# Seven products for k-pairs 2 and 5, token sums made beside their operand, w_mix_out's second half in single blocks, weight splits of 2048 columns

## The chip, the cores and the metric

The kernel runs on one core of a Trainium2 chip. The metric is the device time of one execution in microseconds (us). The kernel before takes 2048.77 us, the median of three runs (2047.95 to 2048.99). The three lie within 1.04 us of one another.

Engines in the profile: PE is TensorE (matmuls), PEld its weight loads, DVE VectorE, ACT ScalarE, POOL GpSimd, SP SyncE, which here only issues transfers.

## The reference

One decoder layer on 256 tokens of 2048 features, with 256 memory tokens, all float32:

```python
hn = rmsnorm(h, norm_mix_w)
q, k, v, g_ret, xr, yr, g_a, g_b = split(hn @ w_in)          # 2048 x 14336
ret_out = silu(g_ret) * head_groupnorm(retention(rotary(q), rotary(k), v))
rnn_out = gelu(yr) * rg_lru(causal_dwconv(xr))
merged = sigmoid(g_a) * (ret_out @ w_proj_ret) + sigmoid(g_b) * (rnn_out @ w_proj_rnn)
h = h + merged @ w_mix_out
h = h + memory_cross_attention(rmsnorm(h), rmsnorm(mem), w_q, w_k, w_v, w_o)
gate, val = split(causal_dwconv(rmsnorm(h) @ w_up))           # 2048 x 11264
h = h + (silu(gate) * val) @ w_down                           # 5632 x 2048
return rmsnorm(h, final_norm_w)
```

All weight matrices are used once, for 256 tokens. They make up nearly all of the 388 MB that the profile shows read from HBM.

## The kernel before

**A product in three.** Each operand is split into hi (rounded to fp32r) and lo (the remainder), and a product is hi·hi + lo·hi + hi·lo, three matmuls of 128 x 128 x 512 (`mm`, L235; `products_n` and `rows_of`). The tokens are the stationary operand (128 features x 128 tokens), the weights the moving one (128 features x 512 columns).

**The weight stream.** `weight_plan` (L68) lists the products in order; `weight_stream` cuts each into chunks of 1 MB, four tiles of 128 x 512, which lie in that order in one DRAM array. `prefetch` (L257) issues the load of a chunk on SP into one of three buffers (`raw`) and then its split: ACT writes hi (a cast, L326 or L339), DVE subtracts for lo (L328 or L340). A split is made in halves of two tiles, 1024 columns, each in a buffer of its own (`hi` and `lo`, six of each, PART_BUFS). `chunks` (L360) keeps AHEAD = 2 chunks prefetched beyond the one being multiplied.

**Single blocks.** `steps_n`/`gemm_n` makes one block of 512 columns for both token halves (2 x 128): for 2048 features 16 feature tiles in four chunks, 24 matmuls each, 96 in all.

**Paired blocks.** `steps_pair`/`pair` (L442 to L501) makes two blocks at once, in eight steps, each a k-pair: two feature tiles x two column blocks, one chunk. A step takes the plain eight tile products (24 matmuls), or, where its number is in `seven`, seven products after Strassen's and Winograd's scheme (21 matmuls) on sums of blocks. For these the weights' sums are made by `seven_parts` (L343): split of p1, p3 (1024 columns) and p2 (512), four additions on DVE (L349), then the split of the sums, q, in two halves. The tokens' sums are made by `sums_of` (L421 to L440): g = hi + lo of the operand (DVE, L428), four differences tq of 128 columns (DVE, L436), their split ts (ACT L437, DVE L438). `steps_pair` asks for them up to two steps ahead. The paired stages are, in order: w_proj_rnn, w_in's gate A (GA), w_proj_ret and w_mix_out, two pairs each, with SEVEN = (1, 3, 5); xa_w_o's first pair with SEVEN_O = (3, 5), its other two blocks single; w_down's first two parts (FF_PARTS), two pairs each, with SEVEN.

**Where operands come from.** A result lies with tokens on partitions and is turned for the next product by `by_dma` (L512): ACT copies it into planes of 16-bit halves (pl, L520), SP issues two DMA transposes (pt), and a step or more later ACT joins the planes (f, L533); then `split_pair` (L549) or `split_cols` splits it into the operand of the next product. For w_proj_rnn the operand `rnn` is made in `gelu_y`, for w_proj_ret `ret` in `split_head` (L711), for w_mix_out `merged` in `turn_merged` (L938), for xa_w_o `osp` in `split_block` (L1044), for w_down `hid` in `gate_up` (L1104), after the convolutions (L1088, L1090). `residual` (L964) runs w_mix_out and xa_w_o and turns each block into the operand of the next stage; during w_mix_out it also squares and splits the memory tokens (`memory_steps`, L608). `pending`/`later` (L356) runs such work after a given number of steps.

**Order.** The program is written in a frame that assigns an order to each engine's instructions, by their dependencies and priorities; matmuls keep the order of the program. On each engine instructions are issued in that order, and one that waits holds those behind it.

Of the kernel before, what the change touches and what calls it, by code (L numbers as in the profile page):

```python
# [9 lines left out]
F32 = mybir.dt.float32  # L10
# [22 lines left out]
PART_BUFS = 6  # L33
# [8 lines left out]
SEVEN = (1, 3, 5)  # L42
# [25 lines left out]
def weight_plan():  # L68
# [81 lines left out]
def hybrid_layer(  # L150
# [106 lines left out]
    def prefetch(n):  # L257
        while len(ahead) < n and taken[0] < len(stream):
# [56 lines left out]
            parts = []  # L315
            for k in range(0, nk, KH):
                if own:
                    xs[k2 + k // KH]
                hi = wp.tile([P, KH, BW], F32R, tag="hi", bufs=PART_BUFS, name=nm("hi"))
                lo = wp.tile([P, KH, BW], F32R, tag="lo", bufs=PART_BUFS, name=nm("lo"))  # L320
                for cs in (slice(k, k + 1), slice(k + 1, k + 2)) if i < 4 else (slice(k, k + KH),):
                    ds = slice(cs.start - k, cs.stop - k)
                    if i == 0 and cs.start == 0:
                        dve.tensor_copy(hi[:, ds], raw[:, cs, :])
                    else:
                        act.copy(hi[:, ds], raw[:, cs, :])  # L326
                    with tc.issue_after(split[cs.start]) if i == 0 else nullcontext():
                        dve.tensor_tensor(  # L328
                            out=lo[:, ds], in0=raw[:, cs, :], in1=hi[:, ds].bitcast(F32), op=ALU.subtract
                        )  # L330
                parts.append((hi, lo))
            ahead.append(((row, c), parts))

    def weight_parts(src):

        n = src.shape[1]
        hi = wp.tile([P, KH, BW], F32R, tag="hi", bufs=PART_BUFS, name=nm("hi"))
        lo = wp.tile([P, KH, BW], F32R, tag="lo", bufs=PART_BUFS, name=nm("lo"))
        act.copy(hi[:, 0:n], src)  # L339
        dve.tensor_tensor(out=lo[:, 0:n], in0=src, in1=hi[:, 0:n].bitcast(F32), op=ALU.subtract)  # L340
        return [(hi[:, i, :], lo[:, i, :]) for i in range(n)]

    def seven_parts(raw):  # L343

        b12, b11, b22, b21 = (raw[:, i, :] for i in range(4))
        p1, p3 = weight_parts(raw[:, 1:3])
        (p2,) = weight_parts(raw[:, 3:4])
        for o, a, b in ((b11, b12, b11), (b12, b12, b22), (b22, b11, b22), (b21, b22, b21)):
            dve.tensor_tensor(out=o, in0=a, in1=b, op=ALU.add)  # L349
        q3, q1 = weight_parts(raw[:, 0:2])  # L350
        q2, q4 = weight_parts(raw[:, 2:4])
# [40 lines left out]
    def steps_n(w, row, st, nk, col):  # L392
# [3 lines left out]
        for k0, n, parts in chunks(nk, w, row, col):  # L396

            def tile_(tt, kk):
                k = k0 + kk
                hi, lo = (t[:, kk % KH, :] for t in parts[kk // KH])  # L400
# [20 lines left out]
    def sums_of(t):  # L421

        if id(t) not in token_sums:
            g = big([P, 2, 2, P], s="g")
            o = big([P, 2, 4, P], F32R, s="ts")
            s = tmp("tq").rearrange("p a (b n) -> p (a b) n", b=2)
            flat = g.rearrange("p j i n -> p j (i n)")
            dve.tensor_tensor(  # L428
                out=flat, in0=t[:, :, 0:S].bitcast(F32), in1=t[:, :, S:BW].bitcast(F32), op=ALU.add
            )  # L430
            (a11, a21), (a12, a22) = ([g[:, j, i, :] for i in range(2)] for j in range(2))
            for d, a, b, op in (
                (0, a21, a22, ALU.subtract), (2, a11, a21, ALU.subtract),
                (1, s[:, 0, :], a11, ALU.subtract), (3, a12, s[:, 1, :], ALU.add),
            ):
                dve.tensor_tensor(out=s[:, d, :], in0=a, in1=b, op=op)  # L436
            act.copy(o[:, 0], s)  # L437
            dve.tensor_tensor(out=o[:, 1], in0=s, in1=o[:, 0].bitcast(F32), op=ALU.subtract)  # L438
            token_sums[id(t)] = (t, o)
        return token_sums[id(t)][1]  # L440

    def steps_pair(w, row, st, nk, c1, c2, seven=SEVEN):  # L442
# [14 lines left out]
        for k0, n, parts in chunks(nk, w, row, (c1, c2, seven)):  # L457
            k2 = k0 // KH
            for i in seven:
                if k2 < i <= k2 + 2:  # L460
                    sums_of(st[i])
# [5 lines left out]
            if k2 in seven:  # L467
# [5 lines left out]
                s1, s2, s3, s4 = ((ts[:, 0, i, :], ts[:, 1, i, :]) for i in range(4))  # L473
# [14 lines left out]
            else:  # L488
                end = k0 + n == nk
                for b, names in enumerate((("p2", "p4"), ("x3", "n"))):  # L490
                    hi, lo = parts[b]
# [767 lines left out]
```

## Time and profile before

| | us |
|---|---|
| median of three runs | 2048.77 |
| the profiled execution | 2047.84 |
| its span, first to last instruction | 2046.1 |
| PE busy in the span | 1991.3 |
| DVE busy | 1542.0 |
| ACT busy | 1343.0 |
| mean granted TensorE clock | 0.987 of full |

The profile is one execution on the chip. Its groups give an instruction's line, operation, tiles (written <- read), shape, count, busy time, mean ns of one, then the idle time of the engine just before and what ended it. Windows cut the span into stretches and give the busy time of each engine, the granted clock, the share of DMA and GB/s. Waits name the instruction that an engine waited for. In the paired stages the windows used below are one pair each: w_proj_rnn 554.6 and 596.1, GA 637.6 and 685.1, w_proj_ret 726.6 and 770.6, w_mix_out 816.0 and 883.5, and the first pairs of w_down at 1502.3 and 1770.8 (1555.2 is a second pair of w_down).

### The profile page before, as it was taken

The numbers are of one execution on the slowest core, as the hardware profiler recorded it, in microseconds if no ns is written. First come the engines' busy times: TensorE is split into PE (matmuls) and PEld (weight loads), VectorE is DVE, ScalarE is ACT, GpSimd is POOL, SyncE is SP. The second block draws the span as 40 slices with busy tenths as digits, with TensorE's granted clock in tenths as the row PEclk, the third lists the DMA queues.
The fourth block names the chain that finished last, engine by engine and source line by source line (L and its number), as shares of the span: only waits on it lengthen the run. The fifth ranks groups of instructions, "written<-read, shape, count | busy, mean of one in ns | idle before, by whom it ended". The sixth has DMA issues, their size and how long they took to land.

```text
span 2046.1 us, 23900 instructions
## 1 busy us (share of the span) xinstructions
PE 1991.3 (97%) x8840; PEld 1643.7 (80%) x8840; DVE 1542.0 (75%) x2029; ACT 1343.0 (66%) x1615; POOL 25.3 (1%) x25
## 2 busy tenths in 40 slices
PE   9999999999999999699999999999989999899998
PEld 8888888888887877577888888888877888788887
DVE  6857766998699999787555568666789676897675
ACT  7647548988454656678666667777765567654773
POOL 0000001000000000000000000000000000000000
PEclk9999999999999999799999999999999999999999
DMA  8755656665555556567766656767655677556773
GB/s 324 249 198 183 227 185 208 205 234 196 185 193 191 190 212 202 199 205 242 228 203 206 208 185 216 227 197 224 226 157 197 211 215 226 187 183 220 226 226 124
DMA packets 197188, 425.60 MB, mean 208 GB/s; under 512 B 142032, under 2 KB 146640, under 8 KB 152016
## 3 DMA queue, kind: packets, MB, share of 16 engines
q1 hardware_dynamic: 197072, 424.09, 62.8%
q8 instruction: 69, 1.13, 0.2%
q14 instruction: 47, 0.39, 0.1%
HBM read 388.39 MB, written 2.10 MB: 191 GB/s over the span
## 4 chain that ended last, share of the span: by engine, by line
PE 80%; DVE 9%; ACT 5%; issue 3%; DMA 2%; POOL 0%; POOLq 0%; SPq 0%; DVEq 0%; ACTq 0%
PE acc L235 72%; PE sm L235 8%; DVE lo L340 3%; DVE raw L349 2%; DVE lo L328 2%; ACT hi L326 1%; ACT f L533 1%; ACT hi L339 1%; DMA pt<-pl 1%; DMA raw<-in_wall 1%; ACT pl L520 1%; ACT s L579 0%; DMA nat<-in_mem 0%; DVE s L580 0%; DVE fv L1090 0%
## 5 line engine op out<-in xcount | busy, mean ns | idle before, releaser
L235 PE MATMUL acc<-hi,s 128*128 128x512 f32 (+1 forms) x4812 | 1481.4, 389 | 1.8 <-ACT hi L326 0.8
L235 PEld LDWEIGHTS acc<-hi,s 128*128 128x128 f32 x4812 | 903.3, 188 | 189.3 <-ACT s L579 1.5
L328 DVE TENSOR_TENSOR lo<-raw,hi 128x1024 fp32r<-128x1024 f32 (+1 forms) x640 | 770.8, 1224 | 358.0 <-ACT hi L326 349.4
L235 PE MATMUL acc<-lo,s 128*128 128x512 f32 (+1 forms) x2406 | 935.8, 389 | 2.4 <-DVE lo L340 1.8
L326 ACT CAST hi<-raw 128x1024 fp32r<-128x1024 f32 (+1 forms) x639 | 651.0, 1044 | 270.4 <-PE acc L235 189.5
L235 PEld LDWEIGHTS acc<-lo,s 128*128 128x128 f32 x2406 | 453.3, 188 | 97.9 <-DVE lo L340 3.2
L339 ACT CAST hi<-raw 128x1024 fp32r<-128x1024 f32 (+1 forms) x152 | 140.9, 942 | 166.5 <-DVE raw L349 111.5
L533 ACT COPY f<-pt 128x1024 uint16<-128x1024 uint16 x128 | 168.4, 1353 | 74.7 <-DMA pt<-pl 74.6
L340 DVE TENSOR_TENSOR lo<-raw,hi 128x1024 fp32r<-128x1024 f32 (+1 forms) x152 | 162.5, 1087 | 26.7 <-ACT hi L339 25.4
L235 PE MATMUL sm<-hi,s 128*128 128x512 f32 x528 | 162.6, 389 | 0.6 <-ACT hi L326 0.6
L520 ACT COPY pl<-rows 128x1024 uint16<-128x1024 uint16 x100 | 99.6, 1043 | 53.2 <-DVE rows L546 40.2
L235 PEld LDWEIGHTS sm<-hi,s 128*128 128x128 f32 x528 | 99.0, 188 | 21.4 <-ACT hi L326 1.0
L349 DVE TENSOR_TENSOR raw<-raw 128x512 f32<-128x512 f32 x152 | 104.4, 687 | 1.5
L235 PE MATMUL sm<-lo,s 128*128 128x512 f32 x264 | 102.8, 389 | 0.5 <-DVE lo L328 0.5
L235 PE MATMUL acc<-hi,ts 128*128 128x512 f32 x228 | 77.2, 423 | 3.5 <-ACT hi L339 3.4
L235 PE MATMUL sm<-hi,ts 128*128 128x512 f32 x76 | 28.6, 441 | 34.8 <-ACT ts L437 29.4
L235 PEld LDWEIGHTS acc<-hi,ts 128*128 128x128 f32 x228 | 47.0, 208 | 15.2 <-ACT hi L339 4.9
L235 PEld LDWEIGHTS sm<-lo,s 128*128 128x128 f32 x264 | 49.6, 188 | 11.3 <-DVE lo L328 1.0
L546 DVE TENSOR_SCALAR rows<-acc,ro 128x512 f32<-128x512 f32 x76 | 53.3, 744 | 4.2 <-PE acc L235 4.2
L1090 DVE SCALAR_TENSOR_TENSOR fg<-f,pf,fg 128x255 f32<-128x255 f32 (+1 forms) x88 | 37.6, 478 | 22.3 <-ACT fg L1088 22.0
L235 PEld LDWEIGHTS sm<-hi,ts 128*128 128x128 f32 x76 | 15.0, 197 | 43.4 <-ACT ts L437 32.3
L235 PE MATMUL acc<-lo,ts 128*128 128x512 f32 x114 | 47.5, 417 | 2.1 <-DVE lo L340 2.1
(179 smaller groups left out, 1008.6 us busy)
## 6 DMA issues: line engine op xcount, KB each, us to landing
raw<-in_wall SPq DMA_DIRECT2D x352, 1024.0 KB, 4.8
nat<-in_x SPq DMA_DIRECT2D x8, 512.0 KB, 9.3
raw<-in_wall SPq DMA_DIRECT2D x7, 512.0 KB, 5.7
pt<-pl SPq DMA_TRANSPOSE x128, 3.2
nat<-in_mem SPq DMA_DIRECT2D x4, 512.0 KB, 9.7
xt<-in_x_t SPq DMA_DIRECT2D x3, 512.0 KB, 9.1
xt<-in_mem_t SPq DMA_DIRECT2D x3, 512.0 KB, 7.0
dec<-in_consts SPq DMA_DIRECT2D x2, 512.0 KB, 4.3
```

The lines of the kernel that those rows point to most:

```text
L235: tc.keep_in_program_order(pe.matmul(*a, **k))
L326: act.copy(hi[:, ds], raw[:, cs, :])
L328: dve.tensor_tensor(out=lo[:, ds], in0=raw[:, cs, :], in1=hi[:, ds].bitcast(F32), op=ALU.subtract)
L339: act.copy(hi[:, 0:n], src)
L340: dve.tensor_tensor(out=lo[:, 0:n], in0=src, in1=hi[:, 0:n].bitcast(F32), op=ALU.subtract)
L349: dve.tensor_tensor(out=o, in0=a, in1=b, op=ALU.add)
L520: act.copy(planes[:, tt], words[:, tt])
L533: act.copy(halves_[:, :, :, cs], turned_[:, :, :, cs])
L546: dve.tensor_scalar_mul(rows[:, tt, :], a[:, tt, :], r[:, tt : tt + 1])
L1090: dve.scalar_tensor_tensor(out=y[:, s:S], in0=z[:, j, 0 : S - s], scalar=pf[:, 2 - s, t : t + 1], in1=y[:, s:S], op0=ALU.mult, op1=ALU.add,)
```

## The change

- SEVEN goes from (1, 3, 5) to (2, 5): two seven-product steps per pair. SEVEN_O stays (3, 5).
- w_mix_out's second half (column blocks 2 and 3) is made as two single blocks.
- PART_BUFS goes from six buffers of two tiles to three of four tiles. A plain chunk of a pair is split by one cast and one subtraction of 2048 columns; of a seven-product chunk p1, p3, p2 are split at once (1536 columns), q in two halves as before. Chunks of single blocks are still split in halves, in one buffer.
- `sums_of` takes the operand's unsplit source, where there is one, instead of adding hi and lo; it uses three subtractions (256, 128 and 128 columns) for four. `with_sums` makes the sums right behind the operand's split, in `gelu_y`, `turn_merged`, `split_block` for osp and `gate_up`; `split_head` asks for them without the source. `steps_pair` asks up to three steps ahead, for operands that exist by then.

```diff
 RAW_BUFS = 3
-PART_BUFS = 6
+PART_BUFS = 3
 AHEAD = 2
...
 EARLY = [2, 2, 4, 4, 4]
-SEVEN = (1, 3, 5)
+SEVEN = (2, 5)
 SEVEN_O = (3, 5)
...
     plan += [("w_in", 0, NT, O_GB + b * BW) for b in range(4)]
-    for w, c in (("w_proj_rnn", 0), ("w_in", O_GA), ("w_proj_ret", 0), ("w_mix_out", 0)):
+    for w, c in (("w_proj_rnn", 0), ("w_in", O_GA), ("w_proj_ret", 0)):
         plan += [(w, 0, NT, (c + b * BW, c + (b + 1) * BW, SEVEN)) for b in (0, 2)]
+    plan += [("w_mix_out", 0, NT, (0, BW, SEVEN))] + [("w_mix_out", 0, NT, b * BW) for b in (2, 3)]
     plan += [(w, 0, NT, b * BW) for b in range(4) for w in ("xa_w_k", "xa_w_q")]
...
                 continue
-            parts = []
+            hi, lo = part_tiles()
             for k in range(0, nk, KH):
...
                     xs[k2 + k // KH]
-                hi = wp.tile([P, KH, BW], F32R, tag="hi", bufs=PART_BUFS, name=nm("hi"))
-                lo = wp.tile([P, KH, BW], F32R, tag="lo", bufs=PART_BUFS, name=nm("lo"))
+                if isinstance(c, tuple):
+                    if k == 0:
+                        weight_parts(raw, hi, lo)
+                    continue
                 for cs in (slice(k, k + 1), slice(k + 1, k + 2)) if i < 4 else (slice(k, k + KH),):
-                    ds = slice(cs.start - k, cs.stop - k)
                     if i == 0 and cs.start == 0:
-                        dve.tensor_copy(hi[:, ds], raw[:, cs, :])
+                        dve.tensor_copy(hi[:, cs], raw[:, cs, :])
                     else:
-                        act.copy(hi[:, ds], raw[:, cs, :])
+                        act.copy(hi[:, cs], raw[:, cs, :])
                     with tc.issue_after(split[cs.start]) if i == 0 else nullcontext():
                         dve.tensor_tensor(
-                            out=lo[:, ds], in0=raw[:, cs, :], in1=hi[:, ds].bitcast(F32), op=ALU.subtract
+                            out=lo[:, cs], in0=raw[:, cs, :], in1=hi[:, cs].bitcast(F32), op=ALU.subtract
                         )
-                parts.append((hi, lo))
-            ahead.append(((row, c), parts))
-
-    def weight_parts(src):
-
-        n = src.shape[1]
-        hi = wp.tile([P, KH, BW], F32R, tag="hi", bufs=PART_BUFS, name=nm("hi"))
-        lo = wp.tile([P, KH, BW], F32R, tag="lo", bufs=PART_BUFS, name=nm("lo"))
-        act.copy(hi[:, 0:n], src)
-        dve.tensor_tensor(out=lo[:, 0:n], in0=src, in1=hi[:, 0:n].bitcast(F32), op=ALU.subtract)
-        return [(hi[:, i, :], lo[:, i, :]) for i in range(n)]
+            ahead.append(((row, c), (hi, lo)))
+
+    def part_tiles():
+        return [wp.tile([P, KC, BW], F32R, tag=a, bufs=PART_BUFS, name=nm(a)) for a in ("hi", "lo")]
+
+    def weight_parts(src, hi, lo):
+
+        act.copy(hi, src)
+        dve.tensor_tensor(out=lo, in0=src, in1=hi.bitcast(F32), op=ALU.subtract)
 
...
         b12, b11, b22, b21 = (raw[:, i, :] for i in range(4))
-        p1, p3 = weight_parts(raw[:, 1:3])
-        (p2,) = weight_parts(raw[:, 3:4])
+        p_hi, p_lo = part_tiles()
+        q_hi, q_lo = part_tiles()
+        weight_parts(raw[:, 1:4], p_hi[:, 0:3], p_lo[:, 0:3])
         for o, a, b in ((b11, b12, b11), (b12, b12, b22), (b22, b11, b22), (b21, b22, b21)):
             dve.tensor_tensor(out=o, in0=a, in1=b, op=ALU.add)
-        q3, q1 = weight_parts(raw[:, 0:2])
-        q2, q4 = weight_parts(raw[:, 2:4])
+        for c in (slice(0, 2), slice(2, 4)):
+            weight_parts(raw[:, c], q_hi[:, c], q_lo[:, c])
+        p1, p3, p2 = ((p_hi[:, i, :], p_lo[:, i, :]) for i in range(3))
+        q3, q1, q2, q4 = ((q_hi[:, i, :], q_lo[:, i, :]) for i in range(4))
         return [p1, p3, p2, q1, q3, q2, q4]
...
 
-    def sums_of(t):
-
-        if id(t) not in token_sums:
-            g = big([P, 2, 2, P], s="g")
-            o = big([P, 2, 4, P], F32R, s="ts")
-            s = tmp("tq").rearrange("p a (b n) -> p (a b) n", b=2)
-            flat = g.rearrange("p j i n -> p j (i n)")
+    def sums_of(t, src=None, scale=None):
+
+        if id(t) in token_sums:
+            return token_sums[id(t)][1]
+        if src is None:
+            src = big([P, 2, S], s="g")
             dve.tensor_tensor(
-                out=flat, in0=t[:, :, 0:S].bitcast(F32), in1=t[:, :, S:BW].bitcast(F32), op=ALU.add
+                out=src, in0=t[:, :, 0:S].bitcast(F32), in1=t[:, :, S:BW].bitcast(F32), op=ALU.add
             )
-            (a11, a21), (a12, a22) = ([g[:, j, i, :] for i in range(2)] for j in range(2))
-            for d, a, b, op in (
-                (0, a21, a22, ALU.subtract), (2, a11, a21, ALU.subtract),
-                (1, s[:, 0, :], a11, ALU.subtract), (3, a12, s[:, 1, :], ALU.add),
-            ):
-                dve.tensor_tensor(out=s[:, d, :], in0=a, in1=b, op=op)
+        o = big([P, 2, 4, P], F32R, s="ts")
+        s = tmp("tq").rearrange("p a (b n) -> p (a b) n", b=2)
+        a = src.rearrange("p j (i n) -> p (j i) n", i=2)
+        dve.tensor_tensor(out=s[:, 0:2], in0=a[:, 0:2], in1=a[:, 1::2], op=ALU.subtract)
+        dve.tensor_tensor(out=s[:, 2], in0=s[:, 1], in1=a[:, 0], op=ALU.subtract)
+        dve.tensor_tensor(out=s[:, 3], in0=a[:, 2], in1=s[:, 2], op=ALU.add)
+        if scale is None:
             act.copy(o[:, 0], s)
             dve.tensor_tensor(out=o[:, 1], in0=s, in1=o[:, 0].bitcast(F32), op=ALU.subtract)
-            token_sums[id(t)] = (t, o)
-        return token_sums[id(t)][1]
+        else:
+            act.mul(o[:, 0], s, scale)
+            dve.scalar_tensor_tensor(
+                out=o[:, 1], in0=s, scalar=scale, in1=o[:, 0].bitcast(F32), op0=ALU.mult, op1=ALU.subtract
+            )
+        token_sums[id(t)] = (t, o)
+        return o
+
+    def with_sums(out, seven, src, scale=None):
+
+        t = split_pair(src, scale)
+        if len(out) in seven:
+            sums_of(t, src, scale)
+        out.append(t)
 
...
             for i in seven:
-                if k2 < i <= k2 + 2:
+                if k2 < i <= k2 + 3 and (not isinstance(st, list) or i < len(st)):
                     sums_of(st[i])
...
         ret.append(split_cols(f, lambda j: half_gn[:, 2 * h + j : 2 * h + j + 1]))
+        if h in SEVEN:
+            sums_of(ret[h])
 
...
                 dve.tensor_tensor(out=o, in0=xr[0][:, cs, :], in1=f[:, cs, :], op=ALU.mult)
-                rnn.append(split_pair(o, 0.5))
+                with_sums(rnn, SEVEN, o, 0.5)
 
...
         for pr in range(2):
-            merged.append(split_pair(f[:, 2 * pr : 2 * pr + 2, :], 0.5))
+            with_sums(merged, SEVEN, f[:, 2 * pr : 2 * pr + 2, :], 0.5)
 
...
             if not sources:
-                if b == 0 or steps:
-                    sources += pair(w, 0, st, NT, b * BW, (b + 1) * BW, *(() if steps else (SEVEN_O,)))
+                if b == 0:
+                    sources += pair(w, 0, st, NT, b * BW, (b + 1) * BW, SEVEN if steps else SEVEN_O)
                 else:
...
 
-    def split_block(f):
-        return [split_pair(f[:, 2 * pr : 2 * pr + 2, :]) for pr in range(2)]
+    def split_block(f, out, seven=()):
+        for pr in range(2):
+            with_sums(out, seven, f[:, 2 * pr : 2 * pr + 2, :])
+        return out
 
...
         ks = []
-        turned_rows(gemm_n("xa_w_k", 0, ms, NT, b * BW), rsms[0], lambda f: ks.extend(split_block(f)))
+        turned_rows(gemm_n("xa_w_k", 0, ms, NT, b * BW), rsms[0], lambda f: split_block(f, ks))
 
         def query(f):
-            qs = split_block(f)
+            qs = split_block(f, [])
             later(1, lambda: softmax(b, qs, ks))
...
                 )
-        turned_rows(a, None, lambda f: osp.extend(split_block(f)))
+        turned_rows(a, None, lambda f: split_block(f, osp, SEVEN_O))
 
...
 
-    def gate_up(gt, vl, hid):
+    def gate_up(gt, vl, hid, seven):
         for pr in range(2):
...
             dve.tensor_tensor(out=o, in0=o, in1=vl[:, cs, :], op=ALU.mult)
-            hid.append(split_pair(o, 0.5))
+            with_sums(hid, seven, o, 0.5)
 
...
             vl = big([P, 4, S], s="fv")
-            conv_up(FF, b, vl, lambda b=b, vl=vl: gate_up(gts[b], vl, hid.setdefault(b, [])))
+            b0 = max(one[1] for one in ff_plan() if one[0] == "down" and one[1] <= b)
+            seven = tuple(i - 2 * (b - b0) for i in SEVEN) if b0 < sum(FF_PARTS[:2]) else ()
+            conv_up(FF, b, vl, lambda b=b, vl=vl, n=seven: gate_up(gts[b], vl, hid.setdefault(b, []), n))
         else:
```

The hunks left out are the new indices of the wider buffers in `steps_n`, `steps_pair` and `last_down`, and the new order of the four token sums.

More of the change, by code (lines that the diff above doesn't have):

```diff
@@ L490, in steps_pair @@
                 for b, names in enumerate((("p2", "p4"), ("x3", "n"))):
-                    hi, lo = parts[b]
+                    hi, lo = (t[:, b * KH : (b + 1) * KH, :] for t in parts)
                     for tt, name in enumerate(names):
```

8 lines of the change are left out of this document (4 added, 4 removed).

## The prediction

> **What bounds it.** I read the page first, for the engine that is full, and then the windows of each stage of paired blocks, to see where it is not.
>
> ```profile
> span 2046.1 us, 23900 instructions
> PE 1991.3 (97%) x8840; PEld 1643.7 (80%) x8840; DVE 1542.0 (75%) x2029; ACT 1343.0 (66%) x1615; POOL 25.3 (1%) x25
> ```
>
> PE is busy for 97%, so there are two ways to gain: fewer matmuls, or fewer stretches in which matmuls wait or run slowly. The pace without waits stands in one row of the chain of work, and what each stage lost against it in the windows (length, then busy time of PE, PEld, DVE, ACT, POOL; the granted clock; DMA).
>
> ```profile
> 1004.71 43.55 PE acc L235 x192
> ```
> ```profile
> 554.60:596.10 41.50, 41.50 (x184) 34.36 (x183) 40.93 (x58) 24.18 (x28) 0.00 (x0) 1.00 0.55 203
> 596.10:637.60 41.50, 41.50 (x185) 34.38 (x184) 39.37 (x46) 21.76 (x23) 0.00 (x0) 1.00 0.54 203
> 637.60:685.10 47.50, 43.61 (x184) 35.43 (x183) 45.58 (x67) 29.05 (x42) 0.00 (x0) 0.96 0.50 177
> 685.10:726.60 41.50, 41.50 (x185) 34.36 (x184) 40.69 (x55) 24.32 (x29) 0.00 (x0) 1.00 0.54 203
> 726.60:770.60 44.00, 42.08 (x185) 34.32 (x184) 42.17 (x60) 25.06 (x30) 0.00 (x0) 1.00 0.53 192
> 770.60:816.00 45.40, 42.78 (x185) 33.96 (x184) 41.46 (x48) 30.89 (x34) 0.00 (x0) 1.00 0.64 198
> 816.00:883.50 67.50, 51.97 (x185) 39.13 (x184) 51.86 (x74) 37.69 (x46) 0.70 (x1) 0.82 0.61 209
> 883.50:932.90 49.40, 45.03 (x185) 35.72 (x183) 42.12 (x57) 39.79 (x57) 0.00 (x0) 0.93 0.67 219
> 1502.30:1555.20 52.90, 44.37 (x184) 35.39 (x183) 51.36 (x77) 31.39 (x37) 0.00 (x0) 0.94 0.55 189
> 1555.20:1596.70 41.50, 41.50 (x185) 34.36 (x183) 38.61 (x43) 22.22 (x24) 0.00 (x0) 1.00 0.59 219
> 1770.80:1822.60 51.80, 45.25 (x185) 36.27 (x184) 50.29 (x76) 31.32 (x37) 0.00 (x0) 0.93 0.54 190
> ```
>
> 192 matmuls in 43.55 us make 0.2268 each. A pair of column blocks has five steps of 24 and three of 21 matmuls, 183 in all, so 41.50 us: four windows show exactly that. The seven others (w_in's gate A first pair, both of w_proj_ret, both of w_mix_out, the first pairs of the two paired w_down stages) exceed it by 6.0, 2.5, 3.9, 26.0, 7.9, 11.4 and 10.3: **68.0 us**. DVE is busy for 93 to 99% of the undisturbed windows: it is as full as PE.
>
> What PE waits for (us in total, times, longest), over the whole span, and then in the second pair of w_mix_out alone:
>
> ```profile
> PE sm L235 <- ACT ts L437: 29.4, 7, 9.2
> PE sm L235 <- DVE ts L438: 5.4, 6, 1.1
> PE acc L235 <- DVE lo L340: 3.9, 5, 1.3
> PE acc L235 <- ACT hi L339: 3.4, 2, 2.6
> ```
> ```profile
> PE acc L235 <- ACT hi L339: 2.6, 1, 2.6
> ```
>
> All four rows are seven-product steps: the token sums (ts) 34.8, the weight parts 7.3, together 42.1. The other 25.9 of the 68.0 is slow matmuls: the clock is 0.82 in the window with the longest waits, 1.00 where there are none. A wait of 1 us thus costs 1.6.
>
> Why the sums are late shows the timeline at the first seven-step of gate A (start, length):
>
> ```profile
> 643.53 2.36 DVE L328 TENSOR_TENSOR lo<-raw,hi 128x1024 fp32r<-128x1024 f32 x2
> 645.80 0.49 DVE L436 TENSOR_TENSOR tq<-g 128x128 f32<-128x128 f32 x2
> 646.53 0.29 DVE L436 TENSOR_TENSOR tq<-g,tq 128x128 f32<-128x128 f32 x1
> 646.85 0.62 ACT L437 CAST ts<-tq 128x512 fp32r<-128x512 f32 x1 [2.75 <-DVE tq L436]
> 647.52 0.49 PE L235 MATMUL sm<-hi,ts 128*128 128x512 f32 x1 [3.66 <-ACT ts L437]
> ```
>
> ACT had been idle for 2.75 us and PE for 3.66: the four subtractions stood on DVE behind the weights' splits. ACT is named by the wait, DVE is the cause.
>
> **The change.** Durations of the operations, by form, in 550 to 960 us (busy, mean ns | idle before):
>
> ```profile
> L340 DVE TENSOR_TENSOR lo<-raw,hi 128x1024 fp32r<-128x1024 f32 x72 | 87.7, 1221 | 22.5 <-ACT hi L339 21.9
> L340 DVE TENSOR_TENSOR lo<-raw,hi 128x512 fp32r<-128x512 f32 x24 | 16.4, 685 | 0.1
> L339 ACT CAST hi<-raw 128x1024 fp32r<-128x1024 f32 x71 | 74.4, 1050 | 97.3 <-DVE raw L349 69.7 <-PE acc L235 9.2 <-PE sm L235 7.6
> L339 ACT CAST hi<-raw 128x512 fp32r<-128x512 f32 x23 | 14.2, 615 | 4.3 <-PE sm L235 4.3
> L349 DVE TENSOR_TENSOR raw<-raw 128x512 f32<-128x512 f32 x96 | 65.9, 687 | 1.0
> L428 DVE TENSOR_TENSOR g<-s 128x512 f32<-128x512 f32 x12 | 8.2, 685 | 0.0
> L533 ACT COPY f<-pt 128x1024 uint16<-128x1024 uint16 x16 | 20.8, 1343 | 0.0
> L520 ACT COPY pl<-o 128x1024 uint16<-128x1024 uint16 x8 | 7.9, 1042 | 0.5 <-DVE o L956 0.5
> L608 ACT ACTIVATE nat<-nat 128x1024 f32<-128x1024 f32 x4 | 4.2, 1054 | 10.4 <-DMA nat<-in_mem 10.4
> L934 DVE SCALAR_TENSOR_TENSOR o<-o,o 128x1024 f32<-128x1024 f32 x4 | 4.8, 1218 | 0.0
> ```
>
> *Matmuls.* Eleven pairs with SEVEN lose one seven-step each (+3: 186), and w_mix_out's second half becomes two single blocks (2 x 96 for 183: +9). 33 + 9 = 42, at 0.2268: **+9.5**, all on the path, since PE is.
>
> *DVE.* Two splits of 1024 columns in a row take 2.36 (row at 643.53) and not 2.44: starts lie 1.14 apart, and by the same 0.08 those of 512 columns 0.60. No split of 2048 or 1536 columns is in the trace. Between nothing saved by joining (2 x 1.14 = 2.28) and no cost beyond one split of 1024 (1.22) I take the straight line through 685 and 1221: 2.29 long, 2.21 to the next start; 1.76 and 1.68 for 1536. For ACT's cast the line through 615 and 1050 gives 1.92 and 1.49. Sums: 0.60 (g), some 0.9 (four subtractions, 645.80 to the cast) and 0.60 before, 2.1; the new form has three subtractions, and no g where the operand's source is at hand: 1.4.
> A pair before: 5 x 2.28 + 3 x (1.14 + 0.60 + 4 x 0.60 + 2.28) + 3 x 2.1 = 37.0 of 41.5 us, and 40.9 with the blocks' ends. A pair after: 6 x 2.21 + 2 x (1.68 + 2.40 + 2.28) + 2 x 1.4 = 28.8, and 32.7 with the ends, of 186 x 0.2268 = 42.2: 78%. The sums are moved out of the stage's full stretch, to the DVE work that makes the operand (gate A's operand is old: its sums start up to three steps ahead instead of two), and a stage's first two steps are plain ones, so that the first seven-step comes one step (5.4 us) later. So the waits for sums should go: **-68.0** with the slow matmuls behind them, and I add back what I can name.
>
> *What is late next.* The parts now lie in three buffers of 2048 columns rather than six of 1024, and a seven-step takes two. The chunk after it gets the buffer of the chunk before it, whose last matmul must be over. From then PE has 21 matmuls (4.76) and two of the next step (0.45) until the first lo is needed: 5.21. The cast takes 1.92, the split 2.29, hand-overs some 0.25: 4.46, which leaves 0.75. There are 24 such places (11 x 2, and two in xa_w_o). Whatever else stands ahead there on ACT or DVE for longer is a wait:
> - gate A: about 0.5 behind the gates' 1.2 us products.
> - w_proj_ret's second pair: ACT has four planes of 1.04 and two joins of 1.34 in line, 1.4 late; and in the program's order the next chunk's 2.29 stands ahead of the second half of the seven-step's own split, 1.6: 3.0.
> - w_mix_out's first pair has the same inversion twice (1.5, 1.8), and at the second ACT has two joins and a 1.05 square of mem ahead, 2.6: 5.9.
> - w_mix_out's second half, single blocks: each block's end puts ACT's joins among casts of 1.05: 0 to 3, I take 1.5.
> - w_down's first pairs: the convolutions of the last value block stand ahead of a split; their rows and the transposes':
>
> ```profile
> L1088 ACT ACTIVATE fg<-f,pf 128x256 f32<-128x256 f32 x40 | 21.0, 591 | 0.3
> L1090 DVE SCALAR_TENSOR_TENSOR fg<-f,pf,fg 128x255 f32<-128x255 f32 x40 | 18.3, 479 | 19.8 <-ACT fg L1088 19.8
> ```
> ```profile
> pt<-pl SPq DMA_TRANSPOSE x128, 3.2
> ```
> ```profile
> 1485.21 7.43 DMA pt<-pl
> ```
>
> Four casts of 0.59, two joins of 1.34 and eight products of 0.48 on DVE are 8.9 us, against some 7 us of room: 2.0 each, 4.0 for both stages; up to 8 if a transpose lands after 7.4 us, as one before it did, and not 3.2.
>
> Named: 0.5 + 3.0 + 5.9 + 1.5 + 4.0 = **14.9**. For the slow matmuls behind them, 0.6 x 14.9 = 9 is the upper end and 0 the lower: their longest is 2.6. The window 883.50 to 932.90 had one wait of 2.6, 1.7 in two others, and a clock of 0.93, the gate A window 3.7 and 0.96; most of my waits are shorter, so I take 3.0. For the 24 tight places without a name, and the RG-LRU stage, 0 to 9: 3.0.
> The Trainium skill ("TensorE: Matmul & The Clock Gate", "HAM oscillation — how this bites in real kernels") wants no gaps on PE over about 3.4 us. By it none of the waits left would lower the clock, and the sum would lose its 3.0; the trace doesn't agree, with 0.93 behind a 2.6 us wait.
>
> *Hidden.* The issue queues: SP has the same 535 instructions, with loads started by buffers that are free at nearly the same time; DMA is at 0.50 to 0.67 in these windows, so a load of some us more would be covered, and costs up to 4.8 us if it isn't. Casts on ACT become fewer (1579 instructions to 1448), with ACT at 22 to 40 of 41 to 67 us. The wide casts add no wait but at the places above. The sums made early hold one buffer each in the pool of 29; a shortage would delay whatever takes one next, 0 to 2 us.
>
> **Sum.** 2046.1 + 9.5 - 68.0 + 14.9 + 3.0 + 3.0 = 2008.5 us of span. The profiled execution took 2047.84, 1.74 above its span; the median of the three runs, 2048.77, is 0.93 above that: 2008.5 + 2.7 = **2011**.
>
> **Rivals.**
> - B, half remains: the sums are made early but the splits of the seven-step, 6.4 us of DVE in 4.76 of PE, still come late behind a block's end. For it: DVE at 99% in 554.60:596.10, and its ends (the 1.22 products of L934) keep their order. Against: 78% by count. Half of 68.0 stays: 2046.1 + 9.5 - 34.0 + 2.7 = 2024.
> - C, all waits go and none of the named ones comes: 2046.1 + 9.5 - 68.0 + 2.7 = 1990. Against: the three inversions are in the order of the instructions.
> - D, slower: the chunk after a seven-step. If in each of the 24 places one other split of 2.29 stands ahead, it is 2.29 - 0.75 = 1.54 late, 37 us in all: 2048, the point from which it decides. With a join of 1.34 ahead too, 2.9 late and 69 us: 2080. For it: 0.75 is thin, and a 2.29 us split can't be cut. Against: in the order of instructions only the three places above have one ahead.
> - E, the change doesn't do what it says: the sums aren't ready earlier because the scheduler leaves their subtractions behind the splits. The waits stay, the matmuls come: 2058. Against: the operand's source is ready a stage earlier, and the order shows the sums directly behind the operand's split.
> - F, the waits left don't lower the clock, most being short: 2008.5 - 3.0 + 2.7 = 2008, inside the forecast. Against: 0.93 in 883.50:932.90. This is what the Trainium skill's section named above would give.
>
> **Chances.** Forecast .40 and F .12; B .20; C .08; D .15; E .05. The range reaches from C's 1990, over the unknown costs of the forecast (+9 for the tight places, +6 for slow matmuls, +4 for transposes, 2030), past B, to 2036; D and E, .20, are left out. Within 0.2%, some 4 us, which is about what a measurement can tell from no change, lies a part of D: .04. Faster .80, slower .16.
>
> **What would show it.** The waits for ts (34.8) gone or under 5; windows of pairs at 42.2, with DVE under 80%; clock 0.97 or more in w_mix_out; waits for lo and hi in the named places of 1 to 3 us. Wrong if ts stays on the list (E), if the chunk after every seven-step waits (D), or if the splits of 2048 columns take other than 2.3 and 1.9 us: each 0.1 more takes from the 0.75.

## The result, and the profile after

The changed kernel takes **2016.57 us**, the median of four runs (2015.44 to 2016.85), against 2048.36 for the kernel before in the same comparison. The ratio is 0.9845, with a 95% interval of 0.9828 to 0.9862: 32 us faster. The forecast was 2011. The profiled execution took 2015.44; its page begins:

```profile
span 2013.6 us, 23001 instructions
PE 1985.5 (99%) x8882; PEld 1645.1 (82%) x8882; DVE 1450.8 (72%) x1781; ACT 1295.0 (64%) x1484; POOL 27.2 (1%) x25
```

42 matmuls more, and PE is busy for less time: it was busy before with slow matmuls. The windows of the paired stages (w_proj_rnn two, w_in's gate A two, w_proj_ret two, w_mix_out's pair and then its two single blocks, w_down's first part two; six of the ten, same columns as before):

```profile
565.40:607.60 42.20, 42.20 (x188) 34.91 (x187) 30.89 (x27) 20.15 (x16) 0.00 (x0) 1.00 0.53 199
...
649.80:691.90 42.10, 42.10 (x187) 34.86 (x186) 38.60 (x44) 22.57 (x22) 0.00 (x0) 1.00 0.53 198
...
776.20:821.40 45.20, 43.22 (x188) 34.63 (x187) 40.22 (x41) 29.94 (x27) 0.00 (x0) 1.00 0.61 207
821.40:878.60 57.20, 46.95 (x187) 36.18 (x186) 39.72 (x43) 34.53 (x37) 2.85 (x1) 0.94 0.68 239
878.60:922.10 43.50, 43.50 (x193) 36.04 (x192) 32.54 (x44) 40.01 (x61) 0.00 (x0) 1.00 0.77 246
1487.70:1530.40 42.70, 42.41 (x187) 34.83 (x186) 36.59 (x39) 26.20 (x23) 0.00 (x0) 1.00 0.61 210
```

186 matmuls at 0.2268 are 42.2 us. Six of the nine pairs are at that floor, the four left out here among them, two within 3.0 of it, and w_mix_out's is still 15.0 over it. (Two more pairs, of w_down's second part, are 0.7 over it together.) DVE is busy for 73 to 94% of the eight pairs other than w_mix_out's; gate A's first, with 38.60 of 42.10 us, has no wait all the same. What PE waits for now:

```profile
PE acc L236 <- DVE lo L341: 6.5, 8, 1.8
PE acc L236 <- ACT s L571: 4.6, 1, 4.6
PE sm L236 <- ACT ti L876: 4.4, 1, 4.4
PE acc L236 <- ACT hi L328: 1.9, 1, 1.9
PE acc L236 <- ACT hi L340: 1.8, 1, 1.8
```

No row names the token sums (ts), which were 34.8 us. Three waits stand where there was next to none before: s, an operand of w_mix_out, and ti (0.2 before) and hi (L328), both in the RG-LRU stage. The widths that no row of before showed:

```profile
L341 DVE TENSOR_TENSOR lo<-raw,hi 128x2048 fp32r<-128x2048 f32 x42 | 95.5, 2289 | 41.3 <-ACT hi L340 41.1
L340 ACT CAST hi<-raw 128x2048 fp32r<-128x2048 f32 x42 | 80.3, 1913 | 50.1 <-PE sm L236 19.7 <-issue 17.2 <-PE acc L236 7.0
```

2289 and 1913 ns, against 2.29 and 1.92 us from the straight line.

### The profile page after: what moved, and what is told of

The parts are those of the page before. It is cut to its first block, busy times and chain, and to the rows that moved or that the text cites. A ratio compares the mean times of both kernels' runs of the same rounds, so it can differ in the third digit from the quotient of the medians.

```text
span 2013.6 us, 23001 instructions
## 1 busy us (share of the span) xinstructions
PE 1985.5 (99%) x8882; PEld 1645.1 (82%) x8882; DVE 1450.8 (72%) x1781; ACT 1295.0 (64%) x1484; POOL 27.2 (1%) x25
## 4 chain that ended last, share of the span: by engine, by line
PE 59%; issue 36%; ACT 2%; DVE 2%; DMA 1%; POOL 0%; SPq 0%; POOLq 0%; DVEq 0%; ACTq 0%
PE acc L236 51%; PE sm L236 8%; ACT hi L340 1%; DVE lo L341 1%; DMA nat<-in_mem 0%; ACT f L548 0%; ACT pl L535 0%; ACT hi L328 0%; DVE raw L350 0%; DVE lo L330 0%; DMA raw<-in_head 0%; DMA pt<-pl 0%; ACT rows L787 0%; DVE s L572 0%; ACT nat L623 0%
## 5 line engine op out<-in xcount | busy, mean ns | idle before, releaser
L236 PE MATMUL acc<-hi,s 128*128 128x512 f32 x4904 | 1508.6, 389 | 6.7 <-ACT s L571 4.6
L236 PE MATMUL acc<-lo,s 128*128 128x512 f32 x2452 | 953.3, 389 | 2.0 <-DVE lo L341 1.7
L330 DVE TENSOR_TENSOR lo<-raw,hi 128x1024 fp32r<-128x1024 f32 (+1 forms) x524 | 621.0, 1216 | 281.8 <-ACT hi L328 281.0
L328 ACT CAST hi<-raw 128x1024 fp32r<-128x1024 f32 (+1 forms) x523 | 522.2, 1043 | 343.9 <-PE acc L236 226.6
L340 ACT CAST hi<-raw 128x2048 fp32r<-128x2048 f32 (+2 forms) x144 | 221.8, 1553 | 195.2 <-PE sm L236 72.0
L341 DVE TENSOR_TENSOR lo<-raw,hi 128x2048 fp32r<-128x2048 f32 (+2 forms) x144 | 262.3, 1844 | 91.5 <-ACT hi L340 91.3
L535 ACT COPY pl<-rows 128x1024 uint16<-128x1024 uint16 x100 | 99.4, 1043 | 14.8 <-DVE rows L559 9.0
L350 DVE TENSOR_TENSOR raw<-raw 128x512 f32<-128x512 f32 x96 | 66.3, 691 | 2.7
L1109 DVE SCALAR_TENSOR_TENSOR fv<-f,pf,fv 128x255 f32<-128x255 f32 (+1 forms) x88 | 37.6, 480 | 20.6 <-ACT fv L1107 20.3
L236 PE MATMUL acc<-hi,ts 128*128 128x512 f32 x144 | 45.4, 397 | 1.9 <-ACT hi L340 1.8
L236 PEld LDWEIGHTS acc<-hi,ts 128*128 128x128 f32 x144 | 27.4, 192 | 8.3 <-ACT hi L340 2.8
```

Of the source, the lines that this page charges most:

```text
L236: tc.keep_in_program_order(pe.matmul(*a, **k))
L328: act.copy(hi[:, cs], raw[:, cs, :])
L330: dve.tensor_tensor(out=lo[:, cs], in0=raw[:, cs, :], in1=hi[:, cs].bitcast(F32), op=ALU.subtract)
L340: act.copy(hi, src)
L341: dve.tensor_tensor(out=lo, in0=src, in1=hi.bitcast(F32), op=ALU.subtract)
L535: act.copy(planes[:, tt], words[:, tt])
```

## The experiments

Two theories stood at the start. **Load**: DVE had no room in the pairs, and one seven-product step fewer gave it some. **Place**: the sums stood behind the splits, and making them with their operand took them out of the way. A third, of the **buffers**, concerns what the changed kernel still loses. With (2, 5) for (1, 3, 5) a stage's first seven-step also comes one step later; the expectations count this as load, and the section on f1 takes the two apart. First each part undone alone in the changed kernel, then each done alone in the kernel before.

### e1_three: three seven-product steps again

```diff
-SEVEN = (2, 5)
+SEVEN = (1, 3, 5)
```

> The changed kernel with seven-product steps 1, 3 and 5 again; all else as changed. Two theories of what removed the waits for token sums. Place: the sums are early now, and that alone is enough; then 33 matmuls fewer, 33 x 0.2268 = 7.5 us, and nothing comes back: 2016.6 - 7.5 = 2009. Load: DVE had no room; three seven-steps bring it from 78% of a pair back to (5 x 2.21 + 3 x 6.36 + 3 x 1.4 + 4) of 41.5 = 92%, and waits return at the first seven-steps of the stages: a third to a half of the former 34.8 us and its slow matmuls, 2009 + 18 to 28 = 2027 to 2037.

2047.25 us, 0.9988 of the kernel before (0.9979 to 0.9998): 29 us of the 32 are gone, more than either theory gave. The sums are early (but for gate A's, which have no source), so place alone fails. The waits:

```profile
PE acc L236 <- DVE lo L341: 21.0, 18, 2.5
...
PE acc L236 <- ACT hi L340: 5.4, 4, 3.2
PE sm L236 <- ACT ts L440: 2.5, 1, 2.5
```

The wait has moved from ts to the weights' own parts, lo above all; those for s and ti grow too, from 4.6 and 4.4 to 7.6 each. Load foresaw waits at the first seven-steps; these stand in and behind seven-steps all over the stages. By the matmul that waits, 14.8 of the 21.0 us are inside a seven-step, most of them at the second half of its own split, and 6.3 in the chunk behind one. That three seven-steps don't go with wide splits, f3 shows below.

### e2_mixpair: w_mix_out's second half as a pair

```diff
-    plan += [("w_mix_out", 0, NT, (0, BW, SEVEN))] + [("w_mix_out", 0, NT, b * BW) for b in (2, 3)]
+    plan += [("w_mix_out", 0, NT, (b * BW, (b + 1) * BW, SEVEN)) for b in (0, 2)]
```

> The changed kernel with w_mix_out's second half as a pair with seven products at steps 2 and 5 again. 6 matmuls fewer than two single blocks: -1.4 us. If single blocks had freed the way into the next stage: the chunk behind a seven-step waits again (the pair had 7.9 us before) and the 3.4 us at the start of xa_w_k and xa_w_q come back, 2020 to 2026. If they bought nothing: 2015.

2020.13 us, 0.9859 (0.9842 to 0.9875), against the changed kernel's 0.9845: some 3 us, within the intervals. Whether single blocks gain anything here stays unclear.

### e3_late: sums made when the pair asks

```diff
     t = split_pair(src, scale)
-    if len(out) in seven:
-        sums_of(t, src, scale)
...
-    if h in SEVEN:
-        sums_of(ret[h])
...
-    if k2 < i <= k2 + 3 and (not isinstance(st, list) or i < len(st)):
+    if k2 < i <= k2 + 2:
```

> The changed kernel with the token sums made again when the pair asks for them, up to two steps ahead, from hi + lo. Place: the sums wait on DVE behind splits and block ends again; half or more of 34.8 us and its slow matmuls: 2016.6 + 28 to 50 = 2045 to 2067. Load: with DVE at 78% two steps (10.9 us) are time enough: 2017 to 2022.

2017.66 us, 0.9846 (0.9832 to 0.9861): the same time. In this kernel place falls as the main cause. Not all waits for sums stay away:

```profile
PE sm L236 <- ACT ts L440: 12.7, 2, 6.5
PE sm L236 <- ACT ti L872: 3.7, 2, 1.9
```

Both of the ts waits are in w_mix_out's pair; the 4.6 us wait for its operand is gone from the list in return. The early sums move that stage's wait, and with these buffers gain nothing on balance.

### e4_halves: splits in halves, six buffers

```diff
-PART_BUFS = 3
+PART_BUFS = 6
...
-        weight_parts(raw[:, 1:4], p_hi[:, 0:3], p_lo[:, 0:3])
+        p1, p3 = weight_parts(raw[:, 1:3])
+        (p2,) = weight_parts(raw[:, 3:4])
```

and the rest of the splitting code as it was before.

> The changed kernel with splits in halves of 1024 columns in six buffers of two tiles again. The joined splits save DVE only about 0.5 us a pair, so by the load theory little is lost: 0 to +3 us. By the buffer theory the remaining waits in the pairs (8 waits for lo, 6.5 us, and one for hi, 1.8 us) and the 1.9 us wait in the RG-LRU stage come from the coarse buffers, and go: 2016.6 - 6 to - 10 = 2007 to 2011. If halves bring waits back because they keep the engines' order worse: above 2020.

**2003.71 us**, 0.9776 (0.9761 to 0.9790): undoing this part gains 14 us, more than I expected from buffers.

```profile
PE acc L236 <- ACT s L569: 6.3, 1, 6.3
PE sm L236 <- ACT ti L874: 3.4, 3, 1.8
...
PE acc L236 <- DVE lo L341: 0.7, 1, 0.7
```

The waits for lo fall from 6.5 to 0.7, and the one for hi of L328 is gone.

### f1_two: only two seven-steps, in the kernel before

```diff
-SEVEN = (1, 3, 5)
+SEVEN = (2, 5)
```

> The kernel before with only SEVEN = (2, 5). 33 matmuls more: +7.5 us. Load theory (DVE full in the pairs): sums still two steps ahead, but one seven-step (6.4 us of DVE) fewer in each pair, and the first one a step later; most of the 34.8 us of waits for sums go: 2048.4 + 7.5 - 40 = 2016 or so. Place theory: the sums still stand behind the splits at a stage's start, half of the waits stay: 2048.4 + 7.5 - 25 to 2056: 2030 to 2056.

2013.92 us, 0.9823 (0.9808 to 0.9839). One line, with 36 matmuls more (twelve pairs, three each), makes the kernel 36 us faster, as was expected under load. That is as much as the whole change gives, or more (0.9845; the intervals overlap).

```profile
PE sm L235 <- ACT ts L437: 12.6, 5, 5.6
PE sm L235 <- DVE ts L438: 3.9, 5, 1.1
```

Of the 34.8 us of waits for ts 16.5 stay, 10.9 of them in w_mix_out; gate A and w_proj_ret have none. The busy time of DVE (third of the engines) in 550 to 1000 us, before and here:

```profile
550.00:1000.00 450.00, 419.52 (x1767) 337.83 (x1766) 393.25 (x519) 285.06 (x354) 1.40 (x2) 0.96 0.59 203
```
```profile
550.00:1000.00 450.00, 437.50 (x1910) 359.64 (x1909) 365.71 (x463) 287.39 (x353) 1.40 (x2) 0.98 0.62 215
```

DVE has less to do, but the waits at a stage's first seven-step fall for another reason. There PE asks for the sums 6.3 us after the stage's start in the kernel before and 11.6 to 11.7 us here, one step later. The first cast of sums (ts, on ACT) that this step needs ends so long after the stage's start (us):

| stage | kernel before | here |
|---|---|---|
| gate A | 9.9 | 5.4 |
| w_proj_ret | 7.0 | 9.8 |
| w_mix_out | 15.4 | 17.2 |
| w_down, first part | 12.9 | 12.6 |
| w_down, second part | 11.7 | 11.7 |

In four of the five stages the sums are no more than 0.3 us earlier, or they are later; PE only asks later. In gate A they are earlier, but those of before would have been in time too. For the last row, the stage starts at 1770.8 before and at 1741.6 here:

```profile
1781.89 0.62 ACT L437 CAST ts<-tq 128x512 fp32r<-128x512 f32 x1 [1.95 <-DVE tq L436]
```
```profile
1752.72 0.62 ACT L437 CAST ts<-tq 128x512 fp32r<-128x512 f32 x1 [0.59 <-DVE tq L436]
```

The 5.5 us that PE waited for the first of these casts are gone. Gate A's first pair has no wait here with DVE still busy for 39.38 of 42.10 us. So at these places the traces speak for the later first seven-step and not for DVE's load. No run has three seven-steps that begin at step 2, or two that begin at step 1, so how the 36 us divide between the two isn't shown.

### f2_mixsingle: only the single blocks, in the kernel before

The edit of e2, the other way, and SEVEN = (1, 3, 5).

> The kernel before with only w_mix_out's second half in single blocks. 9 matmuls more, +2.0 us; the pair's 7.9 us of waits and slow matmuls go, and perhaps the 3.4 us after it: 2048.4 + 2.0 - 7.9 to - 11.3 = 2039 to 2042.5. If the pair's waits only move to the next step: 2050.

2039.55 us, 0.9949 (0.9932 to 0.9965), 10 us: in the profiled executions the half takes 43.5 us in place of 49.4, and the two blocks behind it 43.5 in place of 47.0.

### f3_wide: only the wide splits and three buffers, in the kernel before

The edit of e4, the other way.

> The kernel before with only three buffers of four tiles and splits of 2048 and 1536 columns. Load theory: DVE gains 0.5 us in a pair of 41.5, nothing to see: 2044 to 2049. Buffer theory: the chunk after each of 38 seven-steps has 0.75 us of room and DVE is full, so most of them are late by some tenths of a us up to 1.5: 2048.4 + 10 to + 50 = 2058 to 2098.

2068.16 us, 1.0086 (1.0071 to 1.0101): 18 us slower.

```profile
PE sm L235 <- ACT ts L439: 18.6, 6, 8.5
PE acc L235 <- DVE lo L340: 17.5, 12, 1.8
PE sm L235 <- DVE ts L440: 9.8, 6, 2.2
```

The waits for lo grow from 3.9 to 17.5, while DVE has less to do (381 of 450 us against 393). More work on DVE is thus not the reason; what the edit changes is that the work comes in long pieces into few buffers. Of the 17.5 us 13.3 are inside a seven-step and 4.2 in the chunk behind one. The RG-LRU stage, which has no seven-step, is slower too: w_proj_rnn starts at 564.8 us in place of 554.6.

### f4_sums: only the early sums, in the kernel before

The edit of e3, the other way, with `sums_of` and `with_sums` as changed.

> The kernel before with only the token sums made beside their operand (and three steps ahead where there is no source). Place theory: the waits for ts, 34.8 us, go with their slow matmuls, and only those for the parts stay: 2048.4 - 45 to - 55 = 1993 to 2003. Load theory: the same DVE work in the same stages, somewhat less of it; the wait moves from ts to lo: -10 to -25, 2023 to 2038.

2032.64 us, 0.9912 (0.9895 to 0.9929): 18 us faster, as load has it. The waits for ts fall to 3.8, all of it at gate A, whose sums have no source and still start with the pair; others grow:

```profile
PE acc L235 <- ACT s L568: 9.0, 1, 9.0
PE acc L235 <- DVE lo L340: 7.9, 12, 1.3
PE acc L235 <- ACT hi L339: 5.5, 5, 1.7
```

All eight together, as us against the version that lacks the edit (ratios times 2048.4):

| part | alone, in the kernel before | undone, in the changed kernel |
|---|---|---|
| two seven-steps | -36 | +29 |
| early sums | -18 | 0 |
| single blocks | -10 | +3 (unclear) |
| wide splits, three buffers | +18 | -14 |

The parts alone add up to -46, the whole gives -32. Three of them remove some of the same waits: without the fourth they give 46 together (e4), of the 64 that they add up to alone. The fourth brings new ones in.

### e5_coarse: three buffers, but splits in pieces

```diff
-                    if k == 0:
-                        weight_parts(raw, hi, lo)
+                    cs = slice(k, k + KH)
+                    weight_parts(raw[:, cs], hi[:, cs], lo[:, cs])
...
-        weight_parts(raw[:, 1:4], p_hi[:, 0:3], p_lo[:, 0:3])
+        for cs in (slice(0, 2), slice(2, 3)):
+            weight_parts(raw[:, cs.start + 1 : cs.stop + 1], p_hi[:, cs], p_lo[:, cs])
```

> The changed kernel with its three buffers of four tiles, but every split of 2048 or 1536 columns made again in pieces of 1024 (and 512). It parts the two halves of what cost some 14 us (halves and six buffers together gave 2003.7). If the cost is the length of the operation (the first lo comes 1.1 us later, and nothing can go between): 2004 to 2006, and the waits for lo (6.5 us) go, but the one in the RG-LRU stage, where no operation is wide, stays. If the cost is the buffer (a piece can only be written when all of the chunk before the seven-step is done): 2013 to 2017, and the waits for lo stay, each shorter by at most 1 us.

2008.87 us, 0.9796 (0.9779 to 0.9813): between. By the ratios some 10 of the 14 us come with the length of the operations (by the medians 7.7); the rest is within the intervals of this run and e4, which overlap.

```profile
PE acc L236 <- ACT hi L328: 2.9, 2, 1.9
...
PE acc L236 <- DVE lo L341: 1.1, 2, 0.7
```

lo is down to 1.1, but hi of L328, the splits of single blocks, still waits for 1.9 us in the RG-LRU stage, where no operation is wide (the other 1.0 is at the kernel's start). That wait is in each of the six kernels with three buffers, and not at that place in those with six. ACT there, in the changed kernel and then in the one before:

```profile
328.53 3.87 ACT L535 COPY pl<-rows 128x1024 uint16<-128x1024 uint16 x4
332.31 3.88 ACT L328 CAST hi<-raw 128x1024 fp32r<-128x1024 f32 x4
```
```profile
326.86 2.00 ACT L326 CAST hi<-raw 128x1024 fp32r<-128x1024 f32 x2
328.76 1.71 ACT L770 ACTIVATE rows<-rc,ro 128x256 f32<-128x256 f32 x4
330.37 1.98 ACT L520 COPY pl<-rows 128x1024 uint16<-128x1024 uint16 x2
```

With six buffers two casts go between the planes; with three they stand behind all of them, 5.4 us later.

The traces also tell where the 14 us are, since the changed kernel, e4 and e5 have the same 8882 matmuls in the same order. In the profiled executions the changed kernel falls 14.0 us behind e4: 7.5 in the RG-LRU stage, 3.0 in w_proj_ret's second pair, 2.5 in w_mix_out's pair, the rest in xa_w_o and w_down. e5 wins back what lies in the pairs and nothing in the RG-LRU stage (w_proj_rnn starts at 565.4, 558.1 and 567.7 in the three). So the length of the operations costs in the pairs and the three buffers cost in the RG-LRU stage, some 7 us each by these executions. (In its profiled execution e5 is 4.8 us faster than the changed kernel: 2.2 lost up to w_proj_rnn, 7.1 won behind it.)

### g1_twosingle: two seven-steps and single blocks, nothing else

The edits of f1 and f2 in the kernel before.

> The kernel before with SEVEN = (2, 5) and w_mix_out's second half in single blocks, nothing else: no early sums, splits in halves. Load theory: both parts add, 2048.4 - 36.5 - 10.9 or, as the first has taken part of the second's gain, 2003 to 2010; the early sums of the version with halves (2003.7) then gain 0 to 6 us. Place theory: without early sums 2015 or more.

2012.61 us, 0.9817 (0.9802 to 0.9831), against 0.9823 of f1: beside two seven-steps the single blocks gain nothing that can be seen. e4 has the early sums on top of this, and 0.9776: with splits in halves they gain 8 us. Their waits for ts, 13.3 and 3.6 here, are gone in e4.

### g2_mem: e4, and the squares of the memory four steps later

In w_mix_out's pair ACT stood still in the changed kernel:

```profile
844.69 1.06 ACT L623 ACTIVATE nat<-nat 128x1024 f32<-128x1024 f32 x1 [7.75 <-DMA nat<-in_mem]
...
845.75 2.50 ACT L548 COPY f<-pt 128x1024 uint16<-128x1024 uint16 x2
848.28 1.15 ACT L571 ACTIVATE s<-f 128x512 fp32r<-128x512 f32 x2
```

The join f and the operand s, for which PE waits 4.6 us, stand behind a square that waits 7.75 us for the load of mem.

```diff
-                later(c, lambda c=c: sum_squares(mnat[c], ss, c))
-            later(4, lambda: rsms.append(rstd_rows(ss)))
+                later(c + 4, lambda c=c: sum_squares(mnat[c], ss, c))
+            later(8, lambda: rsms.append(rstd_rows(ss)))
```

> The changed kernel with halves and six buffers, and the squares of the memory tokens four steps later. If ACT holds the joins of merged behind a square that waits for the load of mem (7.3 us idle on ACT, 6.3 us wait of PE, 9.5 us with slow matmuls): the wait goes, 2003.7 - 8 to - 10 = 1994 to 1996. If the joins were waiting for their transposes anyway: 2001 to 2004. If the squares wait elsewhere at their new place: 2000 or more.

2000.45 us, 0.9759 (0.9744 to 0.9773), only 3 us from e4 and within the intervals. The join starts at 826.28, right behind the casts, and s is no longer waited for: the square was what held it. But a step on, PE now waits for hi (3.6 of the 4.9 us; the other 1.3 were there in e4):

```profile
PE acc L236 <- ACT hi L340: 4.9, 2, 3.6
```
```profile
ACT hi L340 <- DMA raw<-in_wall: 6.4, 2, 5.4
```
```profile
raw<-in_wall SPq DMA_DIRECT2D x3, 1024.0 KB, 12.8
nat<-in_x SPq DMA_DIRECT2D x4, 512.0 KB, 6.6
nat<-in_mem SPq DMA_DIRECT2D x4, 512.0 KB, 9.6
```

(waits of PE; waits of ACT from 810 to 850 us; the transfers from 815 to 845 us.) The four loads of x and four of mem, 4 MB, go out on SP ahead of the next chunks, which then land after 12.8 us instead of 4.8, the median of all chunks. For 13 us the profile then shows 382 to 453 GB/s, against means of 198 to 246 in the windows of the result. Another answer than the three that were expected: the wait moved from the square to the weights behind the same loads.

### g3_best: and w_proj_rnn with three seven-steps and its sums late

```diff
+SEVEN_R = (1, 3, 5)
...
-                with_sums(rnn, SEVEN, o, 0.5)
+                rnn.append(split_pair(o, 0.5))
...
-        pair("w_proj_rnn", 0, rnn, NT, b * BW, (b + 1) * BW)
+        pair("w_proj_rnn", 0, rnn, NT, b * BW, (b + 1) * BW, SEVEN_R)
```

> As the one with later squares, and for w_proj_rnn three seven-product steps again (1, 3, 5: 6 matmuls fewer, -1.4 us) with its token sums made in the pair and not in the RG-LRU stage, where PE waits 3.4 us for ACT's ti. If those sums made the waits for ti: 1994 - 1.4 - 3.4 = 1989 to 1991. If not, or if the pair now waits for its sums as gate A's did: 1994 to 2000.

**1993.34 us**, 0.9728 (0.9712 to 0.9744): the fastest, 23 us below the changed kernel. The two parts of the edit weren't run alone.

```profile
PE acc L237 <- ACT hi L341: 5.3, 2, 4.4
PE sm L237 <- ACT ti L875: 0.2, 1, 0.2
```

The waits for ti, 3.4 before it, are 0.2: with six buffers it was the early sums of rnn that had brought them in. The buffers alone bring in as much (3.7 in f3 and in e3, where the sums are late). What is left is the wait behind the loads of x and mem.

## Why the prediction was right

The forecast of 2011 was 5.6 us too low; in span, 2008.5 against 2013.6, 5.1. Term by term:

- **+9.5 for matmuls**: right. Pairs take 42.2, the two blocks 43.50.
- **-68.0**: right as a sum; no wait for ts is left. Its reason was three at once: less DVE work, a first seven-step one step later, and sums made with their operand. The first two together (f1) take 36 us alone, the third 18 (8 where f1's and f2's edits are there too, with splits in halves), and in the changed kernel the third can go at no cost. Of the first two, the later step is what f1's traces show at the first seven-steps; the count of 78% for DVE was the weaker argument. Its sign, DVE under 80%, came true in three of the nine pairs only, and gate A's pairs have no wait at 92 and 94%. The count also took sums for every pair, though a stage makes them once (12 casts of ts for the eight pairs in 550 to 960 of the kernel before).
- **Gate A 0.5**: 0. **w_proj_ret 3.0**: 45.20 - 42.2 = 3.0, of which 1.8 is the inversion (1.6 foreseen) and no row shows the 1.4 for the planes: right in size, in part by luck. **Single blocks 1.5**: 0. **w_down 4.0**: 1.2 (42.70 - 42.2, and 0.7 in the other part).
- **w_mix_out 5.9**, and 3.0 for slow matmuls: 15.0 together. The inversions came as foreseen. What failed is "a 1.05 square of mem ahead": the price was the square's own length, though its row, quoted with it, said 10.4 us idle for the load of mem. In the kernel before that load was late too, but PE had lost 9.2 us just ahead of it to a wait for ts (until 831.46) and then ran at 0.78 of full clock, so that only waits of 0.5 (lo) and 1.1 (ts) were left for what stood behind the square. With the first wait gone, the next late thing was that row. The sign "clock 0.97 or more in w_mix_out" failed with it: 0.94.
- **Tight places and the RG-LRU stage, 3.0**: 10.8. Three of the 24 places, the chunk behind a seven-step, wait, 0.9 us in all, most of it already in w_down's term, so rival D didn't come true here. In e1 and f3, with three seven-steps, such waits for lo are 6.3 and 4.2; the greater part of their 21.0 and 17.5 is the other thing that the prediction named, the next chunk's split ahead of the seven-step's own second half. The RG-LRU stage took the 10.8: w_proj_rnn starts at 565.4 us instead of 554.6, after the same matmuls. Its waits are 1.9 and 0.2 behind the planes (buffers) and 4.4 for ti, the rest slow matmuls. Either part alone brings about the same: w_proj_rnn starts at 564.8 with the wide splits and three buffers (f3), at 563.3 with the early sums (f4). The sum had 3.0 for both, without naming either.
- **Left unchanged: the step into the cross attention.** It gained 3.5 (the windows of its first two blocks, before and after):

```profile
932.90:956.20 23.30, 22.48 (x98) 17.89 (x97) 16.42 (x25) 18.64 (x31) 0.70 (x1) 1.00 0.68 215
956.20:979.90 23.70, 22.38 (x97) 17.84 (x96) 17.46 (x21) 20.01 (x25) 0.00 (x0) 1.00 0.80 263
```
```profile
922.10:943.90 21.80, 21.80 (x98) 18.03 (x97) 16.11 (x25) 18.17 (x29) 0.69 (x1) 1.00 0.82 270
943.90:965.60 21.70, 21.70 (x97) 18.00 (x96) 12.05 (x12) 13.36 (x14) 0.00 (x0) 1.00 0.72 241
```

Added back were 20.9 (14.9 + 3.0 + 3.0); what came is 0 + 3.0 + 15.0 + 0 + 1.2 + 10.8 = 30.0, less the 3.5: 26.5, and 0.4 less in small waits elsewhere: some 26, 5.1 too much. Two terms were 16.9 too low (w_mix_out 9.1, the RG-LRU stage 7.8), the others together some 11.8 too high, so that the sum comes so near is partly luck. The size of the terms for ACT was off: all the added waits above their price (w_mix_out's join, the planes, ti) are ACT's queue, and I had counted DVE's work and only listed ACT's.

The prediction charged the wide splits with "no wait but at the places above". Undone, they give 14 us. That the chunk behind a seven-step has 0.75 us of room was not the point: half of the 14 lies in the RG-LRU stage, where nothing was charged and the three buffers are the cause, and most of the rest in the pairs of w_proj_ret and w_mix_out, where e5's shorter pieces win it back.

## What to carry to other kernels

Before a stage's first step that needs prepared operands, leave room for the preparation: giving PE 36 matmuls more, so that this step comes 5.4 us later and DVE has less to do, paid 36 us. How busy the other engine is doesn't decide alone: pairs with DVE at 93 to 99% ran without a wait here, and where PE waited, the sums came late behind the stage's start. Joining operations saves next to nothing where their price is a straight line in the columns, and takes away the places in the queue where a short, urgent one could stand. When a large wait goes, look in the rows at hand for what has long been late behind it: here a load that ACT waited 10.4 us for.

## What the runs showed of the hardware

The clock falls behind waits of very different length. The 4.6 us wait in the changed kernel's w_mix_out came, with five of 0.7 to 1.8 around it, with 0.94, waits of up to 1.8 in w_proj_ret (776.20 to 821.40) with 1.00, but the one wait of 1.9 in the RG-LRU stage with 0.97:

```profile
318.00:371.00 53.00, 50.84 (x228) 41.59 (x227) 36.05 (x45) 46.13 (x62) 3.67 (x2) 0.97 0.68 209
```

The Trainium skill ("TensorE: Matmul & The Clock Gate", "HAM oscillation — how this bites in real kernels") asks for no gap on PE over about 3.4 us. The trace doesn't agree: right behind the wait of 1.9 us, which ends at 333.40, two matmuls take 1.03 us where two took 0.61 ahead of it, so for such short gaps the measurement decides.
